# Cached sample keys of the third head group: copied once through memory into rows of 4 KB

## Chip, core and metric

The kernel runs on one core of one Trainium2 chip. The metric is device time in microseconds of one execution. Before the change: median 1408.12 us of 3 runs (1403.95 to 1409.54).

## What is computed

One inference step of a decoder layer for a prompt of 1024 tokens and a sample batch of 8 sequences with 8 new tokens each. The part that matters here is the attention of the sample tokens in the third head group (window 2048, dilation 16), over a cache of 2048 rows per sequence:

```python
ATTN_PATTERNS = ((128, 1), (512, 4), (2048, 16))       # (window, dilation) of the three head groups
HEADS_PER_GROUP, HEAD_DIM, DEC_BATCH, DEC_SEQ = 4, 64, 8, 8

def dilated_attention_sample(q, k_full, v_full, dil, band):
    B, T, H, Dh = q.shape
    Lw = k_full.shape[1] - T
    idx = Lw + jnp.arange(T)[:, None] - jnp.arange(band + 1)[None, :] * dil
    valid = idx >= 0
    idxc = jnp.maximum(idx, 0)
    kg = k_full[:, idxc].astype(F32)
    vg = v_full[:, idxc].astype(F32)
    s = jnp.einsum('bthd,btjhd->bthj', q.astype(F32), kg) * (HEAD_DIM ** -0.5)
    p, lse = masked_softmax_stats(s, valid[None, :, None, :])
    return jnp.einsum('bthj,btjhd->bthd', p, vg), lse
```

With a dilation of 16 and 8 new tokens, no two sample tokens read the same cached row: each of the 64 (token, sequence) pairs has 128 cached keys of its own. The rest of the layer is one input projection (pooling branch, q, k, v and two gates), attention of the prompt in three groups, a pooling branch, the merge, and a two-matrix feed-forward part.

## The kernel before

**Stages.** The program runs through: the pooling projection (lines 328, 363), then the q, k and v projections of the three groups in the order g = 2, 1, 0 (function `qkv_part`), then gates, merge and feed-forward. The code counts groups from 0, so g = 2 is the third group. Within a group the tokens come in 8 blocks of 128 prompt tokens and a block 8 with the 64 sample tokens, in the order (8, 0), 1, 2, 3, 4, 5, (6, 7). Each `qkv_part` is one matmul series into one PSUM bank (`pq`, `pk`, `pqk` for q and k together, `pv`); four banks named acc take turns. Prompt attention of earlier blocks (scores `sg`, transposes `tq` and `tp`, outputs `po`) and the pooling branch are woven between the projections.

**Norms.** Behind each q or k projection come squares on ScalarE (ACT, L647, for g = 2 with a running sum into `ms`; for the other groups L643, and VectorE reduces at L644), then on GpSimd (POOL) an addition (L650, `ms`) and a power (L651, `mr`), then ACT scales the projection by `mr` into `qk` (L656). The transposes of `qk` (L672, `tqg2b`) and the next use of the bank wait for that scaling.

**The third group's sample keys.** They are not done with matmuls but by `sample_own_keys`, in pieces. `cache_kv3` is laid out as 2048 rows x 8 sequences x 512 numbers (256 of the key, 256 of the value). A piece takes KPC = 4 of the keys of each half: a tile of 128 partitions (64 pairs, twice) x 4 x 256 numbers, two tiles taking turns. Key pieces are named `pck`, value pieces `pcv`, 16 of each. Each piece is loaded on the SP queue by two transfers of 64 partitions (L846), of which every partition reads four rows of 1 KB, 256 KB apart. POOL multiplies a key piece by the queries `qs` in four instructions (L856), and VectorE (DVE) reduces it (L869). One step of this generator is taken with each projection of g = 1 and g = 0, so the pieces run from 167 to 377 us.

**Order.** TensorE's order is the order in which the code is written. The other engines' and queues' orders are set by a scheduler that estimates times. `behind_pe(ins)` lets an instruction start only once the last projection matmul issued so far has ended; it paces transfers and vector work. POOL's queue carries, besides its arithmetic, only the copies of the caches into the outputs (L2115), which come after 454 us. All other transfers are on SP's queue.

Of the kernel before, what the change touches and what calls it, by code (L numbers as in the profile page):

```python
# [7 lines left out]
F32 = mybir.dt.float32  # L8
# [7 lines left out]
P = 128  # L16
D = 1024
SEQ = 1024
NB, NT = 8, 8
# [7 lines left out]
DIL = (1, 4, 16)  # L27
HD = 64
KPC = 4
# [8 lines left out]
def decoder_step(ctx, tc, i, o):  # L38
    nc = tc.nc
    v_, s_, g_, t_ = nc.vector, nc.scalar, nc.gpsimd, nc.tensor  # L40
    dma = nc.sync.dma_start
# [73 lines left out]
    def split(dst_hi, dst_lo, src):  # L115
        ins = s_.activation(dst_hi, src, AF.Copy)  # L116
        v_.tensor_tensor(dst_lo, src, dst_hi.bitcast(F32), op=ALU.subtract)  # L117
        return ins
# [35 lines left out]
    def feed():  # L154
        while coming_up and coming_up[0]["key"] in ends_of:
            p = coming_up.pop(0)
            cs = slice(p["a"], p["a"] + 512)
            ins = split(p["wt"][:, 0, cs], p["wt"][:, 1, cs], p["raw"])
            behind_pe(ins, ends_of[p["key"]])
            if p["a"] + 512 == p["width"]:  # L160
                throttle.append(ins)
            ask_ahead()
# [23 lines left out]
    def behind_pe(ins, mm=None):  # L186

        tc.add_manual_dep(ins.ins, (mm or last_mm[0]).ins.name,
                          mybir.DependencyInfo(mybir.DependencyClass.Sync, mybir.DependencyReason.DATA), reason="pace")
# [17 lines left out]
    dp = pool("dram", space=DRAM)  # L207
# [14 lines left out]
    pg_d = dp.tile([8, P, H], F32, name="pg_d")  # L222
    ts_d = dp.tile([4, P, 4, H], F32, name="ts_d")
    new_d = dp.tile([NT, NB, 768], F32, name="new_d")
    so_d = [dp.tile([NT, NB, 4, 66], F32, name=f"so_d{g}") for g in range(2)]

    accs = ExitStack()
# [223 lines left out]
    def flush():  # L451
        while later:
            later.pop(0)()
# [85 lines left out]
    ap = pb.enter_context(tc.tile_pool(name="att", bufs=1, reuse_waits="tile"))  # L539
# [300 lines left out]
    def piece(kv, j, name):  # L840
        t = rr(sp1, [P, KPC, 256], F32, name=f"pc{name}", tag="pc", bufs=2)
        src = i["cache_kv3"]
        for hf in range(2):
            a = bass.AP(tensor=src.tensor, offset=src.offset + (64 * hf + j) * DIL[2] * NB * 512 + kv * 256,
                        ap=[[512, NT * NB], [DIL[2] * NB * 512, KPC], [1, 256]])
            dma(t[64 * hf:64 * hf + 64], a)  # L846
        return t

    def sample_own_keys(qs, wq):
        g = 2  # L850
# [290 lines left out]
    for g in (2, 1, 0):  # L1141
        nq = i["qk_norm"]
        if g == 1:
            assert ("p", 3) in done and "ts" in done
            flush()
            pa.close()
            pam.close()
            ap2 = pb2.enter_context(tc.tile_pool(name="att2", bufs=1, reuse_waits="tile"))
            sp1 = psm.enter_context(tc.tile_pool(name="smp1", bufs=1, side="right", reuse_waits="tile"))
            np_ = psm2.enter_context(tc.tile_pool(name="nat", bufs=1, side="right", reuse_waits="tile"))  # L1150
            sp = psm2.enter_context(tc.tile_pool(name="smp2", bufs=1, side="right", reuse_waits="tile"))

            keys = np_.tile([P, 2048], F32, name="keys", tag="nat")
            rest = keys[:, 3 * 4 * 136:]
            extra = [keys[:, n * 4 * 136:(n + 1) * 4 * 136] for n in range(3)]
            osm = ap2.tile([P, 3, 4, 66], F32, name="osm")
            md = ap2.tile([P, 8, 3, 8], F32, name="md")

            wT = ap2.tile([P, 2 * P], F32R, name="wT")

            def clear():
                behind_pe(v_.tensor_scalar(wT, ident.unsqueeze(1).to_broadcast([P, 2, P]), 0.0, None, op0=ALU.mult))
                for a in range(2):
                    v_.memset(osm[64:, a], 0.0)
                    v_.memset(osm[64:, a, :, 64], -NEG)

            soon(*[lambda: None] * 8, clear)
            qs = sp1.tile([P, 768], F32, name="qs")
            for hf in range(2):
                dma(qs[64 * hf:64 * hf + 64], new_d.rearrange("t b c -> (t b) c"))  # L1170
            wq = sp1.tile([P, 2, 256], F32, name="wq", tag="ss")[:, 0]
            dma(wq, bass.AP(tensor=nq.tensor, offset=nq.offset + 2 * 512, ap=[[0, P], [1, 256]]))
            own_keys = sample_own_keys(qs, wq)
            next(own_keys)
        wrow = ap1.tile([P, 256], F32, name=f"wrow{g}", tag="wrow")
        src_w = bass.AP(tensor=nq.tensor, offset=nq.offset + g * 512 + 256, ap=[[0, P], [1, 256]])
        if g == 2:
            dma(wrow, src_w)
            wts = [(place[0] + j) % 3 for j in range(3)]
            for j in range(3):  # L1180
                panel(i["w_in"][4 + 3 * j], f"qkv2_{j}")
        else:
            wts = next_wts
        for blks in ((8, 0), (1,), (2,), (3,), (4,), (5,)) + (((6, 7),) if g else ((6,), (7,))):

            if g and 6 in blks:
                next_wts = [(place[0] + j) % 3 for j in range(3)]
                for j, after in enumerate((((7, 0, 1), (7, 0, 3), (6, 1, 1), (6, 1, 3)), ((7, 1, 1), (7, 1, 3), (6, 2, 1), (6, 2, 3)),
                                           ((7, 2, 0), (7, 2, 1), (7, 2, 2)))):
                    keys_of = [(g,) + a for a in after] + [(g - 1, 8, 1)] * (j == 2)  # L1190
                    line_up(i["w_in"][2 + 3 * j + g - 1], f"qkv{g - 1}_{j}", *keys_of)
            elif not g and 3 in blks:
                wg_first = line_up(lambda a: gate_quarter(a // 512 % 2, a // 1024), "ga0",
                                   *((0, 7, j) for j in (0, 0, 1, 1)), width=2048)
            tiles = {b: qkv_tiles(f"{g}_{b}", b == 8) for b in blks}

            for js in (((0, 1), (2,)) if blks[0] in (1, 2, 3, 4, 5) else ((0,), (1,), (2,))):
                for b in (blks[::-1] if g < 2 and js == (2,) and 8 in blks else blks):

                    own = g < 2 and (g, b, js) in ((0, 8, (0,)), (0, 8, (1,))) or g < 2 and b < 8 and (g, b, js) not in (  # L1200
                        (1, 7, (1,)), (1, 6, (2,)), (1, 7, (2,)), (0, 6, (0,)), (0, 6, (2,)), (0, 7, (2,)))

                    def middle():
                        step()
                        if own:
                            own_step(1)

                    def quarter(q):
                        ends_of[g, b, js[0], q] = last_mm[0]
                        feed()  # L1210

                    if g == 1 and extra and (1, "keys") in done:
                        extra = []
                        natt = np_.tile([P, 8, 2, P], F32R, name="natt", tag="nat")
                        soon(lambda: in_order(0, (0, 2)), lambda: in_order(0, (4, 6)))
                    wide = len(js) == 2
                    qkv_part(g, wts, b, f"{g}_{b}", tiles[b], js, middle if wide else None,
                             quarter if g and b in (6, 7) else None)
                    feed()
                    if own and not wide:  # L1220
                        own_step(1)
                    if g < 2 and b == 8 and 0 in js:
                        dma(wrow, src_w)
                    if g == 0 and b == 8 and 2 in js:

                        sel = ap0.tile([P, 1024], F32R, name="sel", tag="smp")[:, :12 * HD]
                        pick = lambda a: lambda: behind_pe(v_.tensor_tensor(
                            sel[:, 256 * a:256 * a + 256].rearrange("p (a d) -> p a d", d=HD),
                            ident[:, 4 * a:4 * a + 4].unsqueeze(2).to_broadcast([P, 4, HD]),
                            ident[:, 12 + 4 * a:16 + 4 * a].unsqueeze(2).to_broadcast([P, 4, HD]), op=ALU.add))  # L1230
                        soon(pick(0), pick(1), pick(2))
                    if 2 in js:
                        (sample_block if b == 8 else prompt_block)(g, b, *tiles[b])
                if g == 2 and 8 in blks and js != (0,):
                    start(*((pool_branch(), "p") if 2 in js else (token_sums(), "t")), now=True)
# [274 lines left out]
    for n, (f, a) in enumerate(order):  # L1510
# [5 lines left out]
        t = row_tile(1 + a, f)  # L1516
# [587 lines left out]
    for g, n_rows in ((2, 30), (1, 21), (0, 30)):  # L2104
        src, dst = i[f"cache_kv{g + 1}"], o[f"kv{g + 1}_sample"]
# [111 lines left out]
```

## Time and profile before

| | us |
|---|---|
| median of 3 runs | 1408.12 (1403.95 to 1409.54) |
| profiled execution | 1403.42 |
| its span, first to last instruction | 1401.6 |
| TensorE busy | 1392.2 (99%) |
| VectorE, ScalarE, GpSimd busy | 954.3, 754.5, 236.2 |
| TensorE clock granted | 1.00 |
| projections of g = 2, about | 63 to 158 |
| of g = 1 and g = 0, with the pieces | 158 to 380 |

All figures of the profile are of that one execution. A busy TensorE is close to the bound of the program; idle time of another engine matters only where TensorE waits for it. The row of an engine names line, operation, tile written and tile read; "x24" counts instructions merged into a row; a bracket gives the idle time before it and what ended that.

### The profile page before, as it was taken

How to read it: one execution, taken by the hardware profiler on the slowest of the kernel's cores; microseconds unless marked ns; L12 is line 12 of the kernel's file. 1: busy time of each engine (PE TensorE's matmuls, PEld its weight loads, DVE VectorE, ACT ScalarE, POOL GpSimd, SP SyncE). 2: the span in 40 equal slices, each digit the busy share in tenths (PEclk: the TensorE clock that was granted, in tenths of full speed). 3: DMA queues.
4: the chain of work that ended last, by engine and by line, in shares of the span. 5: the costliest groups of instructions: out<-in, count | busy, mean ns of one | idle time of the engine just before them, and what ended most of it. 6: DMA issues, size and time to landing. Idle time of an engine off the chain costs nothing.

```text
span 1401.6 us, 29306 instructions
## 1 busy us (share of the span) xinstructions
PE 1392.2 (99%) x11101; PEld 1342.7 (96%) x11101; DVE 954.3 (68%) x1714; ACT 754.5 (54%) x1778; POOL 236.2 (17%) x330
## 2 busy tenths in 40 slices
PE   9999999999999999999999999999999999999998
PEld 8988977887999999999999999999999999999998
DVE  7788744776776767875568677665665686664565
ACT  8557766687765323563336455555554544444443
POOL 0722266475500000000010000000000000000100
PEclk9999999999999999999999999999999999999999
DMA  6322788745477767965368668856758987777684
GB/s 215 117 90 102 220 228 215 216 127 144 120 254 232 253 216 250 319 227 179 130 203 285 227 221 269 269 200 210 249 189 287 325 272 261 234 243 231 206 260 168
DMA packets 184540, 303.57 MB, mean 217 GB/s; under 512 B 26567, under 2 KB 90509, under 8 KB 182350
## 3 DMA queue, kind: packets, MB, share of 16 engines
q1 hardware_dynamic: 181326, 258.04, 58.4%
q0 software_dynamic: 3072, 43.65, 9.8%
q8 instruction: 87, 1.43, 0.4%
q14 instruction: 55, 0.45, 0.1%
HBM read 231.55 MB, written 113.73 MB: 246 GB/s over the span
## 4 chain that ended last, share of the span: by engine, by line
PE 93%; DMA 2%; POOL 2%; DVE 1%; ACT 1%; issue 0%; SPq 0%; DVEq 0%; POOLq 0%
PE pz L1297 24%; PE pd L2075 24%; PE pg L1297 12%; PE ph L200 7%; PE pqk L200 5%; PE pab L1297 5%; PE pv L200 4%; PE a L328 3%; PE pq L200 1%; PE pk L200 1%; POOL pcv L856 1%; PE sg0b L689 1%; PE pog0b L722 1%; PE tpg0b L708 1%; POOL mr L651 0%; DMA ts_d<-ts 0%
## 5 line engine op out<-in xcount | busy, mean ns | idle before, releaser
L2075 PE MATMUL pd<-places 128*128 128x272 f32 x2688 | 331.7, 287 | 0.0
L2075 PEld LDWEIGHTS pd<-places 128*128 128x128 f32 x2688 | 331.6, 188 | 0.0
L116 ACT ACTIVATE places<-raw_d 128x544 fp32r<-128x544 f32 (+1 forms) x176 | 110.7, 646 | 162.7 <-DMA raw_d<-z_d 51.4
L117 DVE TENSOR_TENSOR places<-raw_d,places 128x544 fp32r<-128x544 f32 (+1 forms) x176 | 122.6, 712 | 92.4 <-ACT places L116 90.6
L2115 POOL DMA_DIRECT2D out_kv_sample_dram<-in_cache_kv_dram x96 | 47.2, 492 | 790.7 <-ACT places L116 580.9
L1297 PE MATMUL pz<-act,places 128*128 128x280 f32 (+1 forms) x1080 | 139.4, 287 | 0.0
L1297 PEld LDWEIGHTS pz<-act,places 128*128 128x128 f32 x1080 | 135.9, 188 | 0.0
L200 PE MATMUL ph<-act,places 128*128 128x280 f32 (+1 forms) x768 | 96.6, 287 | 0.0
L200 PEld LDWEIGHTS ph<-act,places 128*128 128x128 f32 x768 | 96.0, 188 | 0.1
L1297 PE MATMUL pg<-act,places 128*128 128x264 f32 (+1 forms) x576 | 75.6, 288 | 0.0
L1297 PEld LDWEIGHTS pg<-act,places 128*128 128x128 f32 x576 | 72.6, 188 | 0.6 <-issue 0.3
L1297 PE MATMUL pz<-places,apart 128*128 128x264 f32 (+1 forms) x528 | 67.9, 287 | 0.0
L1297 PEld LDWEIGHTS pz<-places,apart 128*128 128x128 f32 x528 | 66.6, 188 | 0.0
L200 PE MATMUL pqk<-places,act 128*128 128x512 f32 x240 | 60.6, 402 | 0.6 <-ACT qk L656 0.6
L1297 PE MATMUL pz<-act,apart 128*128 128x264 f32 (+1 forms) x456 | 59.2, 287 | 0.0
L1297 PEld LDWEIGHTS pz<-act,apart 128*128 128x128 f32 x456 | 57.5, 188 | 0.3 <-ACT e L1862 0.2
L200 PEld LDWEIGHTS pqk<-places,act 128*128 128x128 f32 x240 | 44.7, 192 | 10.5 <-ACT qk L656 0.8
L651 POOL TENSOR_TENSOR mr<-ms,mhalf 128x4 f32<-128x4 f32 (+2 forms) x39 | 52.9, 1356 | 3.1
L856 POOL TENSOR_TENSOR pck<-pck,qs 128x256 f32<-128x256 f32 x64 | 47.4, 774 | 29.1 <-DMA pck<-in_cache_kv_dram 24.5
L328 PE MATMUL a<-act,places 128*128 128x384 f32 (+1 forms) x288 | 50.3, 332 | 0.9 <-ACT act L306 0.4
L1297 PE MATMUL pab<-ab,places 128*128 128x264 f32 (+1 forms) x384 | 50.4, 286 | 0.0
L328 PEld LDWEIGHTS a<-act,places 128*128 128x128 f32 x288 | 47.5, 188 | 2.8 <-ACT act L306 1.2
(435 smaller groups left out, 2789.3 us busy)
## 6 DMA issues: line engine op xcount, KB each, us to landing
out_kv_sample_dram<-in_cache_kv_dram POOLq DMA_DIRECT2D x72, 480.0 KB, 4.9
raw_d<-z_d SPq DMA_DIRECT2D x112, 272.0 KB
z_d<-t SPq DMA_DIRECT2D x80, 272.0 KB
raw_d<-in_w_down_dram SPq DMA_DIRECT2D x80, 256.0 KB
raw_u<-in_w_up_dram SPq DMA_DIRECT2D x64, 256.0 KB
raw_qkv<-in_w_in_dram SPq DMA_DIRECT2D x36, 256.0 KB
pck<-in_cache_kv_dram SPq DMA_DIRECT2D x32, 256.0 KB
pcv<-in_cache_kv_dram SPq DMA_DIRECT2D x32, 256.0 KB
```

The lines of the kernel that those rows point to most:

```text
L116: ins = s_.activation(dst_hi, src, AF.Copy)
L117: v_.tensor_tensor(dst_lo, src, dst_hi.bitcast(F32), op=ALU.subtract)
L200: last_mm[0] = t_.matmul(out, lhs(a, k), rhs(b, k), start=(j == 0), stop=(j == len(terms) - 1))
L328: last_mm[0] = t_.matmul(pts[m][:, :n], wt[:, a, kk, m * P:(m + 1) * P], act4[b][kk][:, :, part4(c)], start=(p == 0 and kk == 0), stop=(p ...
L651: last_norm[0] = g_.tensor_tensor(r[:n, :H], ms[:n, :H], mhalf[:n, :H], op=ALU.pow)
L689: t_.matmul(sc[e][:, hp, j * P:(j + 1) * P], qT[rows, hp, :], kT[rows, 2 + hp, :], start=True, stop=True)
L708: t_.transpose(tp[:, hp * nk + j, :], sms[e][:, hp, j * P:(j + 1) * P], ident)
L722: t_.matmul(po[e * HD:(e + 1) * HD, hp, :], vr[:, h * HD:(h + 1) * HD], pTs[e][:, hp * nk + j, :], start=(j == 0), stop=(j == nk - 1))
L856: ins = g_.tensor_tensor(out, *others, op=ALU.mult)
L1297: last_mm[0] = t_.matmul(out[c], lhs(*term), rhs(*term, c), start=(first and n == 0), stop=(n == len(terms) - 1), skip_group_check=not first)
L2075: last_mm[0] = t_.matmul(outs(chain[t], Q)[c], A[:, a, t * P:(t + 1) * P], Z[:, b, c], start=(fresh and f == 0 and n == 0), stop=(f == NG ...
L2115: ins = g_.dma_start(d, a)
```

## The change

Sixteen buffers in device memory, `own_d`, each 128 rows of 4 KB, take the keys of one piece each, in the layout of the tile. They are filled by 32 transfers on POOL's queue, two for each piece, which read the same 1 KB rows as the loads did. A generator `own_moves` issues one pair after each projection of g = 2 of a prompt block (16 of the 19 such projections; the last three find it empty), each pair paced behind that projection's matmuls. A key piece is then loaded by one transfer of 128 rows of 4 KB (L845) instead of two. Value pieces are loaded as before.

```diff
+    own_d = [dp.tile([P, KPC * 256], F32, name=f"own_d{n}") for n in range(16)]
...
     def piece(kv, j, name):
         t = rr(sp1, [P, KPC, 256], F32, name=f"pc{name}", tag="pc", bufs=2)
         src = i["cache_kv3"]
+        if not kv:
+            dma(t.rearrange("p n d -> p (n d)"), own_d[j // KPC])
+            return t
         for hf in range(2):
...
+    def own_rows():
+        src = i["cache_kv3"]
+        row = DIL[2] * NB * 512
+        for n in range(16):
+            for hf in range(2):
+                a = bass.AP(tensor=src.tensor, offset=src.offset + (64 * hf + n * KPC) * row,
+                            ap=[[512, NT * NB], [row, KPC], [1, 256]])
+                behind_pe(g_.dma_start(own_d[n][64 * hf:64 * hf + 64].rearrange("p (n d) -> p n d", n=KPC), a))
+            yield
+
+    own_moves = own_rows()
...
                     feed()
+                    if g == 2 and b < 8:
+                        next(own_moves, None)
```

The matmuls on TensorE and their order are the same. Lines from 225 to 840 of the code stand one lower after the change, later ones 16 to 18 lower. In the rows below, a name's last number only tells buffers apart, `ms_2_1` is the sum for block 2 (and `_0` for q alone, `_1` for q and k or k alone), and the bracket lists the semaphores waited for (DMASW are those of POOL's transfers).

POOL during the third group's projections, blocks 1 and 2, before:

```order
L650 TENSOR_TENSOR ms_1_1_1020<-ms_1_1_1020,stats 128x8 [waits Activation_49]
L651 TENSOR_TENSOR mr_1_1_1021<-ms_1_1_1020,mhalf 128x8 [waits Pool_49]
L650 TENSOR_TENSOR ms_2_1_1149<-ms_2_1_1149,stats 128x8 [waits Activation_49]
L651 TENSOR_TENSOR mr_2_1_1150<-ms_2_1_1149,mhalf 128x8 [waits Pool_49]
L650 TENSOR_TENSOR ms_3_1_1291<-ms_3_1_1291,stats 128x8 [waits Activation_49]
```

and after:

```order
L651 TENSOR_TENSOR ms_1_1_1042<-ms_1_1_1042,stats 128x8 [waits Activation_49]
L652 TENSOR_TENSOR mr_1_1_1043<-ms_1_1_1042,mhalf 128x8 [waits Pool_49]
L860 DMA own_d_103<-in_cache_kv_dram 256x1x256 [waits DMASW0_49,PE_49]
L860 DMA own_d_103<-in_cache_kv_dram 256x1x256 [waits DMASW1_49]
L860 DMA own_d_104<-in_cache_kv_dram 256x1x256 [waits DMASW2_49,PE_49]
L860 DMA own_d_104<-in_cache_kv_dram 256x1x256 [waits DMASW3_49]
L651 TENSOR_TENSOR ms_2_1_1175<-ms_2_1_1175,stats 128x8 [waits Activation_49]
L652 TENSOR_TENSOR mr_2_1_1176<-ms_2_1_1175,mhalf 128x8 [waits Pool_49]
```

Four transfers now stand between the norms of two blocks; each also waits for the transfer eight places before it.

ACT at the start of those projections (the sample rows 8 and block 0; `rb_s` belongs to the pooling branch), before:

```order
L375 COPY rb_s<-bcx_825 128x4x96 [waits PE_49]
L656 ACTIVATE qk_8_748<-pq_8_752,mr_8_0_772 64x64 [waits Activation_49,Pool_49]
L656 ACTIVATE qk_8_748<-pq_8_752,mr_8_0_772 64x64 [waits Activation_49] x3
L375 COPY rb_s<-bcx_861 128x4x96 [waits PE_49]
L656 ACTIVATE qk_0_750<-pq_0_792,mr_0_0_818 128x64 [waits Activation_49,Pool_49]
L656 ACTIVATE qk_0_750<-pq_0_792,mr_0_0_818 128x64 [waits Activation_49] x3
L647 ACTIVATE qk_8_748,ms_8_1_853<-pk_8_834 64x64 [waits DVE_49]
```

and after:

```order
L376 COPY rb_s<-bcx_841 128x4x96 [waits PE_49]
L376 COPY rb_s<-bcx_879 128x4x96 [waits PE_49]
L648 ACTIVATE qk_8_764,ms_8_1_871<-pk_8_852 64x64 [waits DVE_49]
L648 ACTIVATE qk_8_764,ms_8_1_871<-pk_8_852 64x64 x3
L657 ACTIVATE qk_8_764<-pq_8_768,mr_8_0_788 64x64 [waits Activation_49,Pool_49]
L657 ACTIVATE qk_8_764<-pq_8_768,mr_8_0_788 64x64 [waits Activation_49] x3
L657 ACTIVATE qk_0_766<-pq_0_808,mr_0_0_834 128x64 [waits Activation_49,Pool_49]
```

The scaling of the sample queries `pq_8` moved behind the squares of `pk_8`. On POOL the first pair (`own_d_99`) stands between `ms_8_0` and `mr_8_0`, ahead of the `mr` that this scaling reads.

POOL at the start of the second group's projections, with the first key piece, before:

```order
L856 TENSOR_TENSOR pck_2073<-pck_2073,qs 128x256 x3
L650 TENSOR_TENSOR ms_8_1_2198<-ms_8_1_2198,stats 64x4 [waits DVE_49]
L651 TENSOR_TENSOR mr_8_1_2199<-ms_8_1_2198,mhalf 64x4 [waits Activation_49,Pool_49]
L650 TENSOR_TENSOR ms_0_1_2252<-ms_0_1_2252,stats 128x4 [waits DVE_49]
L651 TENSOR_TENSOR mr_0_1_2253<-ms_0_1_2252,mhalf 128x4 [waits Activation_49,Pool_49]
```

and after:

```order
L872 TENSOR_TENSOR pck_2121<-pck_2121,qs 128x256 x3
L651 TENSOR_TENSOR ms_0_1_2298<-ms_0_1_2298,stats 128x4 [waits DVE_49]
L651 TENSOR_TENSOR ms_8_1_2244<-ms_8_1_2244,stats 64x4 [waits DVE_49]
L652 TENSOR_TENSOR mr_0_1_2299<-ms_0_1_2298,mhalf 128x4 [waits Activation_49,Pool_49]
L652 TENSOR_TENSOR mr_8_1_2245<-ms_8_1_2244,mhalf 64x4 [waits Pool_49]
```

The norm of the sample keys moved behind that of block 0; on ACT the two scalings change places likewise.

## Prediction

> **What bounds the kernel now.** I read the page first (busy shares, the chain that ended last), then TensorE's own waits over the stretch that the change touches, then busy time in two windows: 66 to 152 us (the third group's projections, where the new transfers are issued) and 160 to 260 us (where the key pieces are multiplied).
>
> ```profile
> span 1401.6 us, 29306 instructions
> PE 1392.2 (99%) x11101; PEld 1342.7 (96%) x11101; DVE 954.3 (68%) x1714; ACT 754.5 (54%) x1778; POOL 236.2 (17%) x330
> ...
> PE 93%; DMA 2%; POOL 2%; DVE 1%; ACT 1%; issue 0%; SPq 0%; DVEq 0%; POOLq 0%
> ```
>
> TensorE (PE) is busy for 1392.2 of 1401.6 us, so in the whole program 9.4 us are not matmul. The next rows are all that TensorE waits for between 55 and 415 us, from the first projections to past the last value piece (us in total, times, longest):
>
> ```profile
> PE pog1b L722 <- ACT pTg1b L711: 1.9, 1, 1.9
> PE pqk L200 <- ACT qk L656: 0.6, 1, 0.6
> PE tpg2b L708 <- ACT smg2b L699: 0.3, 1, 0.3
> ```
>
> That is 2.8 us. The matmuls and their order on TensorE are the same after the change, so faster sample keys can give back no more than this. The 1.9 us stand behind copies into natt that precede pTg1b's copy in ACT's order, and that order is not touched there, so 0.9 us are within reach:
>
> ```profile
> 266.97 1.70 ACT L601 CAST natt<-act 128x256 fp32r<-128x256 f32 x3
> 268.54 0.41 ACT L711 COPY pTg1b<-tpg1b 128x256 f32<-128x256 f32 x1
> ```
>
> Now the two windows:
>
> ```profile
> 66.00:152.00 86.00, 86.00 (x585) 74.97 (x584) 71.90 (x165) 58.77 (x307) 25.52 (x27) 1.00 0.32 103
> 160.00:260.00 100.00, 99.00 (x844) 80.65 (x843) 52.95 (x156) 61.34 (x243) 59.05 (x82) 1.00 0.89 232
> ```
>
> Columns: window, length, busy PE, PEld, DVE, ACT, POOL, granted clock, DMA share, GB/s. Where the new transfers go, TensorE has no gap, POOL is busy 25.5 of 86 us, the DMA engines 0.32. Where pieces are read, the DMA engines are at 0.89 and POOL waits for pieces:
>
> ```profile
> POOL pck L856 <- DMA pck<-in_cache_kv_dram: 24.5, 10, 5.6
> ```
>
> These 24.5 us look like the prize, but POOL is not the bound there: a piece is multiplied where the program's order puts it, and of TensorE's waits only the 0.6 us end on POOL's work (below).
>
> **Removed: 32 piece loads of 256 rows of 1 KB, replaced by 16 of 128 rows of 4 KB.**
>
> ```profile
> L846 SPq DMA_DIRECT2D pck<-in_cache_kv_dram x32: 596/608/1007, 167.0 to 256.5; - x32
> 80.48 0.35 SPq L1138 DMA_DIRECT2D out_kv_prompt_dram<-kw  x1
> q1 hardware_dynamic: 181326, 258.04, 58.4%
> q0 software_dynamic: 3072, 43.65, 9.8%
> ```
>
> The first row gives min/median/max ns of one issue on SP; the second is an issue of 128 rows of 1 KB. A pair costs SP 1.22 us; one issue of 128 rows 0.35 to 0.61. SP saves about 16 x 0.7 = 11 us over 90 us, and nothing on TensorE waits for SP. On the DMA engines the mean packet of q1 takes 0.584 x 16 x 1401.6 / 181326 = 72 ns (1.4 KB), and by bytes both queues take about 50 ns per KB. So 8192 packets of 1 KB occupy each of the 16 engines for 8192 x 72 / 16 = 37 us, 8.4 MB in long rows 8192 x 50 / 16 = 26 us: the share in the second window falls by about 0.1. Saved on the path: nothing by itself.
>
> **Added: 32 transfers on POOL's queue.** They read 8.4 MB in 1 KB rows and write 8.4 MB, 26 to 37 us of every DMA engine by the prices above, in a window with 0.32 x 86 = 28 us in use: 54 to 65 of 86 us. The last pair is let go at the end of the pk projection of block 6 (next fence, first row: 146.2 us), and the first piece is read at 167 us, so landing is covered. What has no cover of that kind is POOL's own time for each issue, X. The trace has only one kind of transfer on POOL (second row):
>
> ```profile
> 143.05 3.13 PE L200 MATMUL pk<-places,act 128*128 128x256 f32 x24
> ...
> L2115 POOL DMA_DIRECT2D out_kv_sample_dram<-in_cache_kv_dram x96: 488/488/717, 454.9 to 1335.0; - x96
> ```
>
> Each moves 3072 / 96 = 32 packets; a new one moves 256. Lower end: X does not grow with the packets, 0.49 us. Upper end: all 488 ns grow with them, 8 x 0.488 = 3.9 us. In between stands SP's own slope, (0.61 - 0.35) / 128 = 2 ns per packet, hence 0.49 + 224 x 0.002 = 0.94 us. [...] The decision hangs on what POOL can carry:
>
> ```profile
> 85.14 0.45 POOL L650 TENSOR_TENSOR ms<-ms,stats 128x8 f32<-128x8 f32 x1 [9.89 <-ACT qk L647]
> 85.67 1.99 POOL L651 TENSOR_TENSOR mr<-ms,mhalf 128x8 f32<-128x8 f32 x1
> 96.38 0.61 POOL L650 TENSOR_TENSOR ms<-ms,stats 128x8 f32<-128x8 f32 x1 [8.72 <-ACT qk L647]
> 97.08 2.00 POOL L651 TENSOR_TENSOR mr<-ms,mhalf 128x8 f32<-128x8 f32 x1
> ...
> 131.50 1.31 POOL L650 TENSOR_TENSOR ms<-ms,stats 128x8 f32<-128x8 f32 x1 [9.38 <-ACT qk L647]
> ```
>
> From block to block is (131.50 - 85.14) / 4 = 11.6 us, of which ms and mr take about 2.7. Four transfers stand between two norms, so the queue keeps up while 4X < 8.9, X < 2.2 us. Within a block the waits are also covered:
>
> ```profile
> 90.62 3.04 PE L200 MATMUL pqk<-places,act 128*128 128x512 f32 x12
> 99.10 1.75 ACT L656 ACTIVATE qk<-pqk,mr 128x64 f32<-128x64 f32 x8 [0.96 <-POOL mr L651]
> 105.69 0.66 PE L672 MATMUL tqg2b<-cst,qk 128*128 128x128 f32 x4
> ```
>
> A pair is let go when the projection ends (93.6 us) and ms is ready at 96.38: 2.8 us. The scaling then ends at 100.85, 4.8 us before the transposes that read it. A pair may take 7.6 us before TensorE waits; the 2.2 binds first. Behind the waiting transfers on POOL stand only ms and mr, and for mr wait ACT's scaling and through it TensorE.
>
> The first pair is tighter: it stands between ms and mr of the sample rows.
>
> ```profile
> 67.00 1.00 POOL L651 TENSOR_TENSOR mr<-ms,mhalf 64x4 f32<-64x4 f32 x1
> 68.04 0.91 ACT L656 ACTIVATE qk<-pq,mr 64x64 f32<-64x64 f32 x4 [0.39 <-POOL mr L651]
> 71.27 0.23 ACT L647 ACTIVATE qk<-pk 64x64 f32<-64x64 f32 x1
> 72.48 0.52 PE L622 MATMUL pv<-places,smp_t 128*128 128x256 f32 x1
> ```
>
> mr now ends at 68.0 + 2X. In ACT's new order the scaling comes after pk's squares, which end at 71.5; with 0.9 us it ends at 72.4, and pv (which takes pq's bank) starts at 72.48. Up to X = 1.75 it costs nothing, beyond it 2(X - 1.75): 0.9 us at 2.2. I put 0 for this term, 0.9 as its upper end below the limit.
>
> **Moved.** At the start of the second group ms and mr of the sample keys now follow those of block 0, on POOL and ACT alike.
>
> ```profile
> 173.94 2.80 POOL L856 TENSOR_TENSOR pck<-pck,qs 128x256 f32<-128x256 f32 x4 [3.34 <-DVE ss L873]
> 177.00 1.00 POOL L651 TENSOR_TENSOR mr<-ms,mhalf 64x4 f32<-64x4 f32 x1
> 178.04 0.91 ACT L656 ACTIVATE qk<-pk,mr 64x64 f32<-64x64 f32 x4 [1.63 <-POOL mr L651]
> 179.00 3.02 PE L200 MATMUL pqk<-places,act 128*128 128x512 f32 x12 [0.59 <-ACT qk L656]
> ```
>
> This is the 0.6 us wait. The other pair ahead costs the scaling 1.2 us; a first piece that lands earlier (its load needs one issue less) gives back 0 to 1.5 us. So -0.3 to +1.2, taken at +0.4. The 0.3 us of tpg2b goes, since DVE's score reduction for it now stands ahead of the scaling of qs: -0.3.
>
> **Sum.** 0 (loads) + 0 (POOL, X below 2.2) + 0 (first pair) + 0.4 - 0.3 = +0.1 us on the profiled execution's 1403.42 us (span 1401.6 and 1.8 around it). That execution is 4.7 us under the median of the runs, 1408.12, and below the lowest of them, so I state the forecast at the median: 1408 us. Its own range is 1402 to 1413: the runs from 1403.95 to 1409.54, less 0.9 us and the last 1.9 should ACT's order be kinder, plus 0.9 + 1.2 and some spread. The runs differ by 0.4%, so 0.5% (7 us) is about what can be told from no change.
>
> [...]
>
> **Rivals.**
>
> *POOL's issues are too long (slower).* Place: POOL's queue from 67 to 150 us. From X = 2.2 us on, each further us costs 32 us, since every norm stands behind four transfers: at 2.8, 32 x 0.6 = 19 us, 1427 us; at 3.9, 54 us, 1462 us. For it: 256 packets against 32, DVE busy 84% of the window, and POOL's own ms between 0.45 and 1.31 us there, a factor of 3 with which 0.94 would become 2.7. Against it: SP's gentle slope, and 488 as both minimum and median over 96 issues. Chance 0.27, of which 0.02 below 7 us.
>
> *The new traffic makes loads late.* If the moves reach past 150 us they meet the second group's weight loads, for which ACT already waits:
>
> ```profile
> ACT places L116 <- DMA raw_qkv<-in_w_in_dram: 14.1, 9, 3.7
> ```
>
> Two or three more waits as long as the longest, ahead of a matmul that needs the weight, are 7 to 11 us: 1417 us. The moves have 80 us for 37. Chance 0.03.
>
> *The waits of 0.9 us go, and ACT's 1.9 with them:* -2.8 us, 1405 us. Against it: the last is ACT's order. Chance 0.05, not told from no change.
>
> *The rows do not arrive faster,* the load being bound by the other traffic on the DMA engines: then POOL still waits for pieces and TensorE still does not, 1408 us; it is within the forecast.
>
> **Chances.** Forecast 0.65: no measurable difference; of it 0.02 may show as faster by spread alone. Faster by over 0.5% needs 7 us, and TensorE has 2.8: 0.02. Slower by over 0.5%: 0.25 + 0.03 = 0.28. Within: 0.63 + 0.02 + 0.05 = 0.70. The range from 1402 reaches up into the first rival to X = 2.9 (+22 us), 1430 us, leaving out about 0.12 above and 0.03 below.
>
> **What would show it.** Right: POOL rows of the new transfers of 0.9 to 1.7 us; TensorE's busy time in 66 to 152 us still full; its waits in 55 to 415 us at 2 to 4 us; piece loads with one issue each; DMA share near 0.7 in the first window and 0.8 in the second; POOL's wait for pieces down from 24.5 us. Wrong: issues above 2.2 us, and with them waits of TensorE for ACT's scaled qk that end on mr, all between 75 and 165 us.

## The result, and the profile after

The changed kernel took 1409.56 us (median of 17 runs, 1408.34 to 1416.07), the kernel before in the same session 1406.22 us (17 runs, 1403.95 to 1409.54). The ratio is 1.0026 (95% interval 1.0017 to 1.0035): slower by about 3.7 us. That lies within the 0.5% and within the range given, but its interval excludes one, and the forecast said no change. The profiled execution took 1409.77 us, against 1403.42 before.

The page of the changed kernel, its head and its two data queues (packets, MB, share of the 16 DMA engines' span):

```profile
span 1408.0 us, 29328 instructions
PE 1395.4 (99%) x11101; PEld 1344.4 (95%) x11101; DVE 955.9 (68%) x1714; ACT 753.8 (54%) x1778; POOL 252.4 (18%) x362
...
q1 hardware_dynamic: 174926, 258.04, 57.1%
q0 software_dynamic: 5632, 52.04, 11.6%
```

TensorE (PE) was busy 3.2 us longer and idle 3.2 us longer (1408.0 - 1395.4 = 12.6, before 9.4). It did not do more work, so part of it ran slower. TensorE's waits between 55 and 415 us in the changed kernel (us in total, times, longest):

```profile
PE pqk L200 <- ACT qk L657: 4.6, 1, 4.6
PE pog1b L723 <- ACT pTg1b L712: 0.6, 1, 0.6
PE tpg2b L709 <- DVE qkTg2b L676: 0.3, 1, 0.3
PE pl L508 <- DVE sta L699: 0.2, 1, 0.2
```

The forecast had put pqk's 0.6 us at +0.4; it became 4.6. The forecast had put pog1b's 1.9 out of reach; it became 0.6. The windows of the prediction, and the new wait with the granted clock about it:

```profile
66.00:152.00 86.00, 85.52 (x578) 74.07 (x577) 70.55 (x157) 56.66 (x301) 40.98 (x57) 1.00 0.59 187
160.00:260.00 100.00, 95.28 (x783) 77.56 (x781) 52.23 (x155) 59.72 (x235) 54.51 (x75) 0.97 0.72 219
184.00:187.00 3.00, 2.78 (x7) 2.20 (x8) 2.34 (x3) 1.68 (x7) 1.57 (x3) 0.50 0.90 335
187.00:190.00 3.00, 3.00 (x13) 1.96 (x13) 0.00 (x0) 0.00 (x0) 1.46 (x3) 0.57 0.59 217
```

The column before the last two is the clock that TensorE was granted. After the wait it is 0.50 and 0.57 for six us. The timeline shows what that cost: the twelve matmuls took 5.49 us, before 3.02.

```profile
184.22 5.49 PE L200 MATMUL pqk<-places,act 128*128 128x512 f32 x12 [4.63 <-ACT qk L657]
```

Aligned by the matmuls (same order in both), TensorE's lag of after behind before, in the two profiled executions, was:

| at (us of before) | lag, us | what lies in between |
|---|---|---|
| 51 | +0.41 | start-up, ahead of any changed code |
| 113 | +1.31 | third group: waits of pl and tpg2b |
| 175 | +1.18 | |
| 179 | +5.22 | pqk's wait, 4.63 for 0.59 |
| 182 | +7.69 | the same matmuls at the lower clock |
| 207 | +7.25 | |
| 270 | +5.82 | pog1b's wait, 0.6 for 1.9 |
| 384 | +6.47 | |

So two losses (third group, start of the second) and one gain (near 269 us) hide in a difference of a few us. These two executions lie 6.4 us apart, the medians 3.3: the rows show where the time went in these two, and what each part is worth in the median is for the experiments. Other rows the prediction asked for: the transfers and piece loads (min/median/max ns of one issue), and POOL's wait for pieces (total, times, longest), down from 24.5 us:

```profile
L860 POOL DMA_DIRECT2D own_d<-in_cache_kv_dram x32: 577/620/744, 67.3 to 148.9; - x32
L845 SPq DMA_DIRECT2D pck<-own_d x16: 319/343/679, 170.6 to 263.1; - x16
```

```profile
POOL pck L872 <- DMA pck<-own_d: 13.7, 4, 4.2
```

### The profile page after: what moved, and what is told of

It is laid out like the page before. It is cut to its first block, busy times and chain, and to the rows that moved or that the text cites. A ratio compares the mean times of both kernels' runs of the same rounds, so it can differ in the third digit from the quotient of the medians.

```text
span 1408.0 us, 29328 instructions
## 1 busy us (share of the span) xinstructions
PE 1395.4 (99%) x11101; PEld 1344.4 (95%) x11101; DVE 955.9 (68%) x1714; ACT 753.8 (54%) x1778; POOL 252.4 (18%) x362
## 3 DMA queue, kind: packets, MB, share of 16 engines
q8 instruction: 87, 1.43, 0.4%
## 4 chain that ended last, share of the span: by engine, by line
PE 94%; DMA 2%; DVE 1%; ACT 1%; POOL 1%; issue 1%; SPq 0%; DVEq 0%; ACTq 0%; POOLq 0%
PE pz L1315 24%; PE pd L2093 24%; PE pg L1315 12%; PE ph L200 7%; PE pab L1315 5%; PE pqk L200 5%; PE pv L200 4%; PE a L329 3%; PE pq L200 2%; PE pk L200 1%; DMA ts_d<-ts 1%; PE sg0b L690 1%; PE pog0b L723 1%; PE tpg0b L709 1%; DMA wq<-in_qk_norm_dram 0%
## 5 line engine op out<-in xcount | busy, mean ns | idle before, releaser
L200 PEld LDWEIGHTS pqk<-places,act 128*128 128x128 f32 x240 | 46.4, 199 | 15.0 <-ACT qk L657 4.9
```

The costliest lines, as they stand in the source:

```text
L200: last_mm[0] = t_.matmul(out, lhs(a, k), rhs(b, k), start=(j == 0), stop=(j == len(terms) - 1))
```

## The experiments

All ratios are against the kernel before, run on the same chip beside them.

### Moves alone, loads alone

**e1_moves.** `piece()` loads from the cache as before; the transfers stay.

```diff
-        if not kv:
-            dma(t.rearrange("p n d -> p (n d)"), own_d[j // KPC])
-            return t
```

> The 32 transfers on POOL are made, but the pieces are loaded from the cache in rows of 1 KB as before, and nothing reads the copy. The order at the second group's start is that of the changed kernel (the norm of the keys of tile 0 ahead of that of tile 8 on POOL, scaling on ACT swapped). Order theory: as slow as the changed kernel, 3 to 5 us over the kernel before, with TensorE idle 3 to 5 us before the places matmuls of pqk near 179 us. Rival, that the loads in 4 KB rows from the fresh copy are what costs: as the kernel before, within 1 us, and no such idle time.

Measured: 1413.77 us, ratio 1.0058 (1.0043 to 1.0072), worse than the change itself. pqk's wait was there (4.2 us), as the order theory had it, but the cost was twice what it allowed. TensorE's lag had grown from 0.73 us at 51 us to 4.88 at 175, ahead of that wait; pqk's wait and the lower clock behind it added 5.3 us, and pog1b's wait near 279 us, again with a lower clock behind it, 2.1. In the timeline of this run, ahead of 175 us:

```profile
95.80 0.55 SPq L534 DMA_DIRECT2D ts_d<-ts  x1
102.45 1.36 DVE L525 TENSOR_TENSOR ts<-act,act 128x544 f32<-128x544 f32 x2 [3.87 <-DMA ts_d<-ts]
103.80 0.42 DVE L676 COPY qkTg2b<-tqg2b 128x256 f32<-128x256 f32 x1
104.36 0.71 PE L690 MATMUL sg2b<-qkTg2b 64*128 64x128 f32 x8 [2.08 <-DVE qkTg2b L676]
```

The pooling branch's store of `ts` (544 KB, on SP's queue) is issued at 95.80 and lets VectorE (DVE) go on at 102.45, 6.65 us later. A pair of the new transfers had been issued at 94.69 and another at 100.20. In VectorE's order the copy of qkTg2b stands behind the waiting `ts`, and TensorE waits for that copy. The same pair of rows in the kernel before:

```profile
92.82 0.55 SPq L533 DMA_DIRECT2D ts_d<-ts  x1
...
96.21 1.36 DVE L524 TENSOR_TENSOR ts<-act,act 128x544 f32<-128x544 f32 x2 [1.08 <-DMA ts_d<-ts]
```

3.39 us from issue to release: beside the new traffic this store took almost twice as long.

**e2_loads.** No transfers; the key pieces are read in rows of 4 KB from the weights `w_in`, so they are other numbers, and the amount of work is the same.

```diff
-            dma(t.rearrange("p n d -> p (n d)"), own_d[j // KPC])
+            dma(t.rearrange("p n d -> p (n d)"), i["w_in"][j // KPC][:, :KPC * 256])
...
-                    if g == 2 and b < 8:
-                        next(own_moves, None)
```

> No transfers on POOL; the key pieces are loaded by one transfer each of 128 rows of 4 KB, from the weights' memory (so the third group's cached keys are other numbers; the amount of work is the same). Order at the second group's start as in the kernel before. Order theory: within 1 us of the kernel before, no idle time of 4 us near 179 us. Rival, that the 4 KB rows gain what the change hoped for: 1 to 3 us faster than the kernel before. Rival, that the 4 KB loads cost: 3 us slower.

Measured: 1402.76 us, 0.9977 (0.9968 to 0.9987), 3.2 us faster. The order theory alone said no gain; the hope of the change, its rival, was right. TensorE's lag falls from +0.73 at 179 us to -1.43 at 270 us, 1.7 us of it at pog1b's wait. (Past 570 us this execution, the slowest of the run's eleven, loses 3.3 us again, at rows that the edit does not touch.) The timeline of ScalarE (ACT) and SP shows what stands ahead of that wait. Before:

```profile
258.72 0.58 SPq L127 DMA_DIRECT2D raw_qkv<-in_w_in_dram  x1
...
265.38 0.63 ACT L116 ACTIVATE places<-raw_qkv 128x512 fp32r<-128x512 f32 x1 [2.23 <-PE pv L200]
...
269.00 0.65 PE L722 MATMUL pog1b<-pTg1b,v 128*64 128x128 f32 x6 [1.93 <-ACT pTg1b L711]
```

With the 4 KB loads:

```profile
258.98 0.58 SPq L127 DMA_DIRECT2D raw_qkv<-in_w_in_dram  x1
...
263.90 0.63 ACT L116 ACTIVATE places<-raw_qkv 128x512 fp32r<-128x512 f32 x1 [2.24 <-DMA raw_qkv<-in_w_in_dram]
...
267.57 0.65 PE L723 MATMUL pog1b<-pTg1b,v 128*64 128x128 f32 x6 [0.26 <-ACT pTg1b L712]
```

ACT's conversion waits for the weight load of the first row (both use the same semaphore) and starts 6.66 us after SP issued it, with 4 KB pieces 4.92. The row of before names pv as releaser, but the load's completion is in the trace, at 265.30 us, 0.08 us ahead of the conversion (263.82 in the other run). Behind the conversion stand the copies into natt and the copy of pTg1b that TensorE waits for.

In all seventeen kernels this interval and pog1b's wait go together: 6.7 to 7.5 us (before, e1, e5, e6, e10) with waits of 1.9 to 2.8 us, and 3.7 to 5.5 us (all others) with 0 to 0.7. The rows of the last key piece issued ahead of the weight load go with them in fifteen of the seventeen: 1 KB rows with the long interval, 4 KB rows with the short one. Two go against it: e4, with 1 KB rows there, had 5.20 us and a wait of 0.51, and e6, with 4 KB rows, 7.09 and 2.35. So it is shown that a late weight load makes this wait. That the 1 KB rows make the load late is likely, but the two exceptions say that something else can do it or undo it, and what that is stays open.

**e5_tiny.** As e1, with almost nothing to carry.

```diff
-                            ap=[[512, NT * NB], [row, KPC], [1, 256]])
+                            ap=[[512, NT * NB], [row, 1], [1, 16]])
```

> The 32 transfers on POOL stay in their places, but each carries 64 rows of 64 bytes instead of 256 KB, and the pieces are loaded from the cache in rows of 1 KB; the copy is not read. With so little to carry, the norms at the second group's start come in the order of the kernel before (tile 8 ahead of tile 0). Theory (the cost is the traffic beside the stores of ts and the order that follows from it): within 1 us of the kernel before; the wait of sg2b near 103 us and the idle 4 us near 179 us both gone. Rival, that it is POOL's issue time or the waits behind PE that cost: 4 to 8 us slower than the kernel before, as the run with the moves alone (1.0058).

Measured: 1405.83 us, 1.0004 (0.9994 to 1.0015). Issuing 32 transfers on POOL, each pair behind a projection, has no cost that can be told; one took 505 ns (median). No wait of sg2b, pqk 0.8 us. Traffic and the order that comes with it are the cost.

### The order at the start of the second group

**e3_first** (of after) and **e4_before_first** (of before) take the first key piece one step later.

```diff
-                        (1, 7, (1,)), (1, 6, (2,)), (1, 7, (2,)), (0, 6, (0,)), (0, 6, (2,)), (0, 7, (2,)))
+                        (1, 0, (0,)), (1, 7, (1,)), (1, 6, (2,)), (1, 7, (2,)), (0, 6, (0,)), (0, 6, (2,)), (0, 7, (2,)))
```

> The changed kernel with the sample's first piece taken one step later, so that on POOL the norms of the keys of tiles 8 and 0 come ahead of it and in the order of the kernel before; all transfers, copies and loads stay. Order theory: the idle time near 179 us is under 1.5 us, the clock stays at 1.00 there, and the time is 0 to 2 us under the kernel before. Rival, that the transfers on POOL or their traffic cost the 3.7 us: still 3 to 4 us over the kernel before.

> The kernel before with the same first piece one step later: the control of the run beside it. Order theory: 0 to 1 us faster than the kernel before (its own 0.6 us of idle time near 179 us goes). Rival, that the step itself is worth several us apart from the transfers: 3 us faster or slower.

Measured: e3 1404.79 us, 0.9998 (0.9985 to 1.0011); e4 1402.62 us, 0.9983 (0.9971 to 0.9995). In e3 pqk waits 0.58 us and the clock stays at 1.00; nothing else was changed in the code, so the first piece ahead of the norms makes the long wait. All of TensorE's waits in e3 between 55 and 415 us:

```profile
PE sg2b L690 <- DVE qkTg2b L676: 1.5, 1, 1.5
PE pv L200 <- DVE places L117: 1.4, 1, 1.4
PE pog0b L723 <- DVE md L699: 0.8, 1, 0.8
PE pqk L200 <- ACT qk L657: 0.6, 1, 0.6
PE pl L508 <- DVE sta L699: 0.5, 1, 0.5
```

But the same step gains 1.7 permille in the kernel before too, more than its 0.6 us of wait: in the trace 0.9 us at 179 us and 1.4 near 269, less 0.9 lost at pog0b near 384. By this control the part of the step that belongs to the change is 2.8 - 1.7 = 1.1 permille, and the intervals leave it open whether that differs from nothing. The control still loads rows of 1 KB, though; e8 below gives one with 4 KB.

**e6_pin.** POOL takes the norm of tile 8 ahead of tile 0's again; the first piece stays ahead of both.

```diff
+            if g == 1 and blk == 0 and js == [1]:
+                behind_pe(eps, last_norm[0])
```

> The changed kernel with one dependency more: in group 1 the norm of the keys of tile 0 waits for that of tile 8, so that POOL takes tile 8 first as in the kernel before; the first piece still comes ahead of both, and all the traffic stays. Theory (the swapped order is the larger part): the idle time before pqk near 179 us falls from 4.6 to 2 to 3 us (one norm, 1.0 us, and one block of scaling, 0.9 us, less), and with it half of the clock's loss: 1406 to 1408 us, 2 to 3 us under the changed kernel. Rival, that the first piece alone makes the idle time: 4 us or more stay, and the time is that of the changed kernel.

Measured: 1407.93 us, 1.0024 (1.0014 to 1.0034). The wait fell as expected and the clock with it stayed whole:

```profile
184.46 3.02 PE L200 MATMUL pqk<-places,act 128*128 128x512 f32 x12 [2.63 <-ACT qk L659]
```

```profile
184.00:188.00 4.00, 3.54 (x21) 2.60 (x21) 1.93 (x8) 3.37 (x17) 3.65 (x5) 1.00 1.05 344
```

The time did not follow: it cannot be told from after's 1.0026. The profiled execution, the longest of its runs, lost 3.7 us near 104 us instead (a wait of sg2b of 2.07 us, then a lower clock), where after's lost nothing, and pog1b waited 2.35 us where after's waited 0.56. What the swapped order of the two norms costs in the median is therefore not settled.

### Traffic: how much, and where

**e14_half** and **e15_double**, both with the later first piece: half the transfers (for the last eight pieces; the others load from the cache), and each transfer made twice.

```diff
-                    if g == 2 and b < 8:
+                    if g == 2 and (js == (2,) and b < 6 or js == (0,) and b in (6, 7)):
```

```diff
+                behind_pe(g_.dma_start(own_e[n][64 * hf:64 * hf + 64].rearrange("p (n d) -> p n d", n=KPC), a))
                 behind_pe(g_.dma_start(own_d[n][64 * hf:64 * hf + 64].rearrange("p (n d) -> p n d", n=KPC), a))
```

**e8_loadsfirst** is e2 with the later first piece: no transfer at all.

> No transfers on POOL; the key pieces are loaded in 128 rows of 4 KB from the weights' memory (other numbers in the third group's cached keys), and the first piece comes one step later. It is what the change could give if the moves were free. Theory (gains of 3.2 us from the loads and 2.4 us from the step lie at different places, the first at 207 to 270 us, the second at 179 us): 4 to 6 us under the kernel before, 1400 to 1402. Rival, that both remove the same wait: 2.5 to 3.5 us under it.

> Half the transfers: the last eight pieces, two transfers after the value part of each of blocks 0 to 5 and after the query part of blocks 6 and 7, first piece one step later; the other pieces from the cache. Theory (cost goes with the traffic beside the third group's stores): between 0.9973 (none) and 0.9998 (all), near 0.9985. Rival (any traffic there costs the same, or the order it brings does): 0.9998 or more.

> Twice the transfers: each of the 32 is made a second time into another scratch that nothing reads, at the same places; first piece one step later. POOL issues 64 of them, and four stand ahead of some norms. Theory (cost goes with the traffic): 1.0020 or more, with VectorE waiting for ts stores over 12 us in the stage (3.9 in the kernel before, about 10 with 32 transfers) and TensorE over 5 us. Rival (the cost does not come from traffic): within 1 us of the run with 32 (0.9998).

| transfers (first piece later) | ratio, interval | DVE waits for ts stores, 60 to 160 us |
|---|---|---|
| 0 (e8) | 0.9973 (0.9965 to 0.9982) | 3.9 us |
| 16 (e14) | 0.9979 (0.9966 to 0.9992) | 5.6 us |
| 32 (e3) | 0.9998 (0.9985 to 1.0011) | 9.6 us |
| 64 (e15) | 1.0143 (1.0122 to 1.0164) | 13.0 us |

From 0 to 32 transfers the cost is 2.5 permille, 3.5 us, clear of the intervals. (e8's pieces come from the weights' memory, e3's from own_d; that this matters is not excluded.) Between 0 and 16 no cost can be told: TensorE does not wait for VectorE in e14, and its extra 1.7 us are no slower store, since the store that VectorE waits for near 155 us takes 5.99 us in e14 and 6.00 in the kernel before, and VectorE only comes to it earlier. e15 is no clean dose: its transfers also stood between ms and mr, and most of its loss is TensorE waiting for scaled qk. The two ends of the last column, e8's row and e15's among VectorE's waits (total, times, longest):

```profile
DVE ts L525 <- DMA ts_d<-ts: 3.9, 4, 1.5
```

```profile
DVE ts L526 <- DMA ts_d<-ts: 13.0, 6, 4.0
```

With e8 the place of the first piece can be weighed once more, at 4 KB rows in all four kernels. Without transfers the later step gains 0.9977 - 0.9973 = 0.4 permille, with them 1.0026 - 0.9998 = 2.8. The 2.4 between are what the early first piece costs once the transfers are there; with the four intervals added in squares, 0.4 to 4.4, just clear of nothing.

**e7_spread.** All 32, but grouped behind the value parts, away from the stores that follow the query and key parts.

```diff
+                    if g == 2 and (js == (2,) and b < 6 or js != (2,) and b in (6, 7)):
+                        for _ in range(2 if b < 6 else 1):
+                            next(own_moves, None)
```

> First piece one step later, and the transfers regrouped: none after the query and key parts of blocks 0 to 5, four after each of their value parts, two after the first two parts of blocks 6 and 7; same 32 transfers. Theory (traffic just ahead of a store of ts makes it land later and holds VectorE): the wait of sg2b near 103 us is under 0.5 us and the time is 1 to 3 us under the run with the first piece later alone (1404.8): 1402 to 1404. Rival, that traffic costs wherever it lies in the third group's stage: 1404 to 1407, with a wait of 1 us or more at another block.

Measured: 1407.21 us, 1.0012 (1.0003 to 1.0021). sg2b's wait fell to 0.60 us, but VectorE waited 11.0 us for the stores in all, and TensorE 2.09 us for pl at 150 us. The rival was right: in this stage the place of the transfers shifts the wait and does not remove it.

**e11_early8** and **e12_early16** move eight or sixteen pieces ahead of the stage, where the kernel before leaves the DMA engines idle (23 to 30 us); later first piece in both.

```diff
         pool_evac(0, c, pool_input(0, wt, c))
+        if c == 1:                      # e12: c == 0
+            for _ in own_rows():        # e11: pieces 8 to 15
+                pass
```

> The last eight pieces are moved at 25 to 35 us and loaded in rows of 4 KB, the first eight from the cache; first piece one step later. Theory (the moves cost what they cost because their traffic lies beside the stores of ts in the third group's stage): no wait of sg2b near 103 us, no wait of pl near 150 us, 1400 to 1402. Rival, that traffic costs wherever it lies: half of what the full moves cost with this step (2.5 permille), about 1403 to 1404.

> All sixteen pieces are moved from about 17 us on, ahead of POOL's sums of x (32 to 47 us in the kernel before); first piece one step later. Theory (the traffic is free away from the third group's stage; POOL's 20 us of issue and 27 us of the DMA engines fit between 20 and 50 us): within 1 us of the run with eight pieces. Rival, that POOL's sums come 5 to 10 us late, or that the loads of the second phase do, and TensorE waits at 41 to 55 us: 3 to 10 us slower than the run with eight pieces.

Measured: 1419.40 us, 1.0098 (1.0081 to 1.0116), and 1422.02 us, 1.0116 (1.0096 to 1.0137). I was wrong on e11: 30 to 40 us were filled (DMA share 0.96 in its first half, 0.99 in its second), POOL was held by the transfers, and TensorE waited 13.85 us for its sums of x (e12: 18.04). POOL's timeline in e12 shows how:

```profile
17.80 4.98 POOL L413 DMA_DIRECT2D own_d<-in_cache_kv_dram  x8 [17.35 <-PE a L329]
23.53 0.58 POOL L413 DMA_DIRECT2D own_d<-in_cache_kv_dram  x1 [0.75 <-DMA own_d<-in_cache_kv_dram]
...
46.38 18.86 POOL L301 TENSOR_TENSOR xs<-xs,xs 128x768 f32<-128x768 f32 x9
```

Eight go out at once; the ninth and several later ones wait for landings, since each waits for the one eight places before it. The nine sums of x begin at 46.4 us and end at 65.2, in the kernel before at 32.1 and 54.4. That late start is only part of TensorE's wait: its reduction started behind the fourth sum in the kernel before (40.4 us) and behind the seventh in e11 and e12, so POOL's order changed as well, and in e11 POOL also waited 3.3 us between the sums for ACT.

### Where the loads' gain lies, and a version that is faster than both

**e9_one** (piece 15 moved early, first piece as in after), **e10_onefirst** (the same, first piece later), **e13_twofirst** (pieces 14 and 15, first piece later): as e11 with another first piece number.

```diff
-        if not kv:
+        if not kv and j // KPC >= 15:   # e13: 14
```

> Only the last key piece (n = 15) is moved, by two transfers on POOL at about 25 us, where the kernel before has the DMA engines idle from 23 to 30 us; it is loaded in rows of 4 KB, the other fifteen from the cache as before. Theory (the loads' gain comes from the last piece, for which POOL waits 2.00 us at 264 us and TensorE 1.93 us at 269 us): that wait falls under 0.5 us, 1402.5 to 1404 (1.2 to 2.4 us under the kernel before). Rival, that the gain of the 4 KB rows is spread over all pieces: within 0.7 us of the kernel before.

> The same single piece moved early, and the sample's first piece taken one step later. Theory: the gain of the 4 KB loads and the later step together, as without any transfer (0.9973): 3 to 4.5 us under the kernel before, about 1401; faster than both kernels. Rival (gain spread over all pieces): as the later step alone, 2.4 us under it.

> The last two key pieces (n = 14, 15) are moved by four transfers at about 26 us, where the DMA engines are idle, and loaded in rows of 4 KB; the others come from the cache; first piece one step later. Theory (the gain lies at the piece that TensorE waits for near 268 us, here the last but one): that wait, 2.60 us with one piece moved, falls under 0.5 us, and the time to the level of all loads in 4 KB rows without moves (0.9973), 3 to 4.5 us under the kernel before. Rival (the gain is spread over all pieces): as the later step alone, 0.9983.

Measured: e9 1405.37 us, 1.0008 (0.9993 to 1.0023); e10 1403.81 us, 0.9984 (0.9970 to 0.9998); e13 1401.71 us, **0.9976 (0.9963 to 0.9988)**. In e9 pog1b's wait fell to 0.62 us (under 0.5 was expected), yet its profiled execution lost 1.26 us at pqk and 1.34 at a transpose near 200 us, and the time is that of the rival: no gain. e10 moved the wrong piece: with the first piece later, the piece ahead of that weight load is number 14, which came from the cache (pog1b waited 2.60 us). e13 has it in 4 KB rows. Its waits near 197, 266 and 383 us are what is left of TensorE's between 42 and 415 us:

```profile
196.86 0.71 PE L722 MATMUL tpg1b<-cst,smg1b 128*128 128x128 f32 x2 [0.38 <-ACT smg1b L713]
266.36 0.65 PE L736 MATMUL pog1b<-pTg1b,v 128*64 128x128 f32 x6 [0.67 <-ACT pTg1b L725]
383.43 1.09 PE L736 MATMUL pog0b<-pTg0b,v 128*64 128x128 f32 x16 [0.83 <-DVE md L712]
```

e13, with four transfers instead of 32, cannot be told from e8, where sixteen pieces cost no transfer (0.9973). e13 and e14 are faster than both kernels, by 3.4 and 3.0 us against before. The later first piece alone (e4) gives 2.4 us of it. That the two pieces add anything to e4 is not shown: the intervals overlap, and in the traces e4's wait at pog1b (0.51 us) was no longer than e13's. e10 with its 2.60 us says only that the later step alone does not always keep this wait short.

## Why the prediction was wrong

The forecast's zero was a sum in which three terms were mis-sized: the transfers' own traffic (not in the sum at all) and the moved order cost more than was put, the loads gained more. The first is the step that failed: the prediction asked only whether the transfers land in time and whether the DMA engines have room, and so put their traffic at nothing. It cost 3.5 us, and 6.9 together with the early first piece, as in the change; the loads gained 3.2. Step by step:

- **New traffic: not in the sum, a rival at 0.03, and the step that failed.** I weighed capacity (28 us in use and 26 to 37 more of 86; measured share 0.59, which is 23 more) and looked for loads after 150 us. What was late were stores of ts inside the window, on which VectorE already waited 3.9 us before the change; I had not asked for VectorE's waits there. Price: 2.5 permille, 3.5 us, with the later first piece (0.9973 to 0.9998; 0.9 to 4.1 permille with the two intervals added in squares). With the early one, as in the change, transfers and order together cost 1.0026 - 0.9977 = 4.9 permille, 6.9 us (after against e2). In after's own profiled execution this stage lost only 1.0 us; e1's lost 3.0 there and e3's 2.5.
- **Loads on the path: 0, wrong.** Without moves they gain 2.3 permille (e2), 3.2 us. The sentence that failed here put pog1b's 1.9 us out of reach because it stands behind ACT's copies and that order is not touched. The order stayed; its start moved, since ACT's conversion ahead of them waits for a weight load that is in flight beside a key piece. I had seen POOL's 24.5 us of waits for pieces, asked only who waits for POOL, and not what else is in flight beside a piece. The 2.8 us that I took for the most the loads could give were read from one execution.
- **POOL's issues: right in the sum.** X was 0.62 us (577 to 744 ns), under my 0.9 to 1.7 and inside 0.49 to 3.9, and 32 issues had no cost that can be told (e5). No run shows the 1.7 us of my upper end: four times the rows (256 against e5's 64) added 0.12 us to 505 ns, 0.6 ns a row. My 256 packets were a misreading, too: q0 gained 2560, which is 80 of 3.3 KB for a transfer of 256 rows. The main rival, at 0.27, rested on these packets, on VectorE busy for 84% of the window and on POOL's own spread. That a busy VectorE makes an issue longer was my guess and is not shown: the longest of the 32 took 744 ns, with VectorE busy for 70.6 of 86 us.
- **First pair: 0, right.** TensorE's lag does not move between 51 and 95 us.
- **Moved: +0.4 in a range of -0.3 to +1.2, wrong in the profiled execution by 6 us.** pqk's wait grew by 4.0 and the clock took 2.5 more. I let POOL's start hang on the first piece's landing, though my own row named VectorE (DVE ss) as what POOL waited for. The chain that ended last shows POOL behind wq, through VectorE, in both kernels. SP issued wq at 169.97 us instead of 166.39, of which 1.2 to 1.5 us are TensorE's lag and the rest is SP's changed order. Before:

```profile
166.39 5.53 DMA wq<-in_qk_norm_dram
...
173.94 2.77 POOL pck L856 x4
...
179.00 3.02 PE pqk L200 x12
```

  After:

```profile
169.97 6.11 DMA wq<-in_qk_norm_dram
...
176.20 0.43 DVE qs L878
...
177.42 2.00 POOL pck L872 x3
...
181.69 0.43 ACT qk L657 x2
...
184.22 5.49 PE pqk L200 x12
```

  That the first piece ahead of the norms makes this wait is shown (e3). What it costs in the median is known only roughly: 2.4 permille, 3.4 us, by the four kernels with 4 KB rows (0.4 to 4.4), and e6 does not settle how much of it is the swapped norms.
- **tpg2b: -0.3, right** in the trace.
- **Sum.** With the measured pieces, in permille: loads -2.3 (e2), traffic +2.5 (e8 to e3), the early first piece with the traffic there +2.4, together +2.6. The range held, and TensorE had no 7 us of waits to give back, as read. (By its own terms the range's lower end is 1403.95 - 0.9 - 1.9 = 1401.2 us, not 1402; nothing hangs on it.) That the net came within 0.3% of zero is in part luck: two losses and a gain, none of them in the sum at its size, nearly cancelled.

## What to carry to other kernels

A transfer that fits into the idle share of the DMA engines can still cost, here 3.5 us (e8 against e3): look for who waits for any DMA in that window, stores included, and for what is queued behind the one who waits. When a load gets cheaper, ask which other transfer beside it lands earlier. And when a kernel is at its bound within 1%, make only the move that a named wait asks for, and try the cheaper step first: two moved pieces could not be told from sixteen that cost no transfer, and taking the first piece later, with no transfer at all, already gave 2.4 of the 3.4 us.

## What the hardware showed unexpectedly

**A wait of a few microseconds can halve TensorE's clock, and its length alone does not decide.** The granted clock behind some of TensorE's waits:

| run, wait ends at (us) | wait, us | granted clock behind it |
|---|---|---|
| e6, 104.28 | 2.07 | 0.50 |
| e1, 104.36 | 2.08 | 1.00 |
| e6, 274.39 | 2.36 | 0.50 |
| e1, 279.23 | 2.52 | 0.50 |
| e6, 184.46 | 2.63 | 1.00 |
| e5, 270.27 | 2.77 | 1.00 |
| e15, 105.45 | 3.35 | 0.51 |
| e15, 172.65 | 3.37 | 1.00 |
| e15, 79.85 | 3.61 | 0.50 |
| e1, 187.54 | 4.24 | 0.50 |
| after, 184.22 | 4.63 | 0.50 |

Two of e15's waits are each ahead of 24 matmuls of the same shape; behind them the row of e6's shortest wait, and a window right after it with the clock in the third column from the end:

```profile
79.85 5.49 PE L200 MATMUL pv<-places,act 128*128 128x256 f32 x24 [3.61 <-ACT qk L658]
...
172.65 3.15 PE L200 MATMUL pv<-places,act 128*128 128x256 f32 x24 [3.37 <-ACT qk L658]
```

```profile
104.28 1.13 PE L692 MATMUL sg2b<-qkTg2b 64*128 64x128 f32 x7 [2.07 <-DVE qkTg2b L678]
```

```profile
105.00:107.50 2.50, 2.50 (x10) 1.89 (x8) 2.50 (x7) 0.00 (x0) 0.00 (x0) 0.50 0.15 52
```

The stretches at 0.50 last 3.41 us (e1, e6) or 6.83 (after, from 182.8 to 189.6 us). The length of the wait does not tell which lose the clock: waits of 2.07, 2.36, 2.52 and 3.35 us lost the clock, and waits of 2.08, 2.63, 2.77 and 3.37 kept it, the first of each list at the same matmuls (sg2b). What decides is not shown. A stall of 4.63 us thus cost 2.5 us more than its own length (after), one of 2.07 us 1.5 more (e6).

**A store can take longer beside POOL's transfers.** The 544 KB store of the rows above took 3.39 us to its release in the kernel before, beside the transfers 4.28 (after), 6.09 (e3) and 6.65 us (e1). Not every store is slowed: the first that VectorE waits for took 3.4 us in before and in after, and the last one 6.00 in the kernel before, with no transfer of POOL in flight. What makes a store slower is not shown.
